# Retention in small steps queued behind Strassen products, the table of angles kept on chip, and part of the rotary sums on VectorE

## The chip, the cores and the metric

The kernel runs on one core of a Trainium2 chip. It is written in Bass with the Tile layer: the program names tiles and instructions, Tile places the tiles, adds the waits between engines, and fixes the order of each engine's instructions when the program is built. The metric is device time in microseconds of one execution. The engines are TensorE (PE; its weight loads PEld), VectorE (DVE), ScalarE (ACT), GpSimd (POOL) and SyncE (SP), which here issues nearly all DMAs.

## The reference

The reference is one inference step of a one-layer streaming encoder on 1024 prompt tokens and 64 sample tokens, 1088 in all, with a model width of 1024, in float32. What matters here is its first part, the input projection and the retention branch:

```
xn = rms_norm(x);  q, k, v, gate, swa_q, swa_k, swa_v, gate_a, gate_b = split(xn @ w_in)
q, k = rope(q), rope(k) / 16                  # 4 heads of 256, halves of 128: x1*cos - x2*sin, x2*cos + x1*sin
per chunk:  s = (q @ k.T) * decay             # inside the chunk
            o = s @ v + (q @ state) * q_decay
            state = state * gamma^C + (k * k_decay).T @ v
a = (rms_norm(o) * silu(gate)) @ w_ret_out
```

The states after the prompt and after the sample are outputs too. Sliding-window attention, the mixing of both branches, cross attention and a gated feed-forward part follow.

## The kernel before

All matmuls that carry float32 data are done in three passes: both operands are split into a high part (a cast on ACT) and a low part (a subtraction on DVE), by `split` at line 122, and high by high, high by low and low by high are summed in PSUM.

**Products.** The input projection goes by pairs of 128 output columns. A pair is one Strassen multiplication (`strassen`, line 247): seven products instead of eight, each of 24 matmuls (`multiply`, line 197) into two PSUM banks (`bank_pair`; three such pairs turn round). The weights are loaded as two raw tiles, POOL forms four sums of their quarters, ACT and DVE split seven results (`weight_ops`, line 166; five tiles for the split weights). DVE forms the running sums u2, u3, u5 and hands each of four quadrants of the result, i the column block and t the half of the tokens, to an `emit` function. Head 0's values are multiplied without Strassen (`plain`).

**What is done with a quadrant.** `project_phase` (line 541) holds four cases. `taken` (line 556) writes the quadrant into the next of eight stage tiles, in turn. `values` stores it to DRAM. `project` multiplies it by the token's inverse root mean square, on POOL, or on DVE where a sigmoid or SiLU on ACT follows. `rotated` (line 581) waits until both column blocks of a token half are there, loads the cosines and sines of that half (a tile `cs` of one buffer, line 590), forms two products with the sines in a tile `ab` and two with the cosines in place, all on DVE (lines 594 to 597), lets POOL subtract and add (lines 598 and 599), and stores both results to `d_qkv`.

**Retention.** `retention` (line 691) works on one head, four blocks of 256 tokens and then the 64 sample tokens. For a block it loads k, v and q from `d_qkv`, transposes k on PE and scales and splits it (`kt`, lines 709 to 715), splits k and q (`ks`, `qs`), transposes v and scales and splits it (`vb`), multiplies k by q (`pss`, line 725), masks and splits the scores (`sf`, `ss`), multiplies `kt` by `vb` (`pkv`, line 737), adds that to the state (line 747), and sums the output `po` from scores and values and from the queries and the old state (lines 748 to 758). `ret_out` (line 793) takes the output's squares on ACT, an inverse root through some small DVE and ACT instructions (`rsqrt`, line 280), scales it (line 808), transposes it back (`pb`, line 812) and stores it to `d_ret`. All of these PSUM tiles, and those of the roots, share two banks (`bank`, line 679, tag "r"). The working tiles, `ks`, `qs`, `vf`, `kt`, `vb`, `sf`, `ss`, `st`, `state` and `o`, have one buffer each.

**The order of the work.** The loop at line 628 goes over the four heads: k and q of the head with their rotation; for head 0 the tokens' squares (`token_squares`), roots (`token_roots`) and the decay tables (`retention_setup`); for the others v and the window queries of the head before (`w_sq`); then the retention of the head. After head 0, `spread_roots` writes the roots along the tokens, after head 1 `bias_table` builds the bias rows of the window attention. Behind the loop come the window keys and values, the last window queries, three sets of gates of four pairs each, and steps of the memory projection between them. That is the order of writing. Each engine's queue is ordered when the program is built, by a timeline of modelled durations: of the instructions whose inputs are ready in it, the one written first goes first. So the retention of a head, written before the next head's products, is ahead of them where it is ready, and they fill the time in which it is not. An engine takes its queue strictly in order on the chip. `issue_after(x)` adds that what is written under it, on the engine of x, comes after x; `in_order` (line 851) does that with the last matmul, and the window attention already uses it.

Of the kernel before, what the change touches and what calls it, by code (L numbers as in the profile page):

```python
# [29 lines left out]
H = 4  # L30
# [79 lines left out]
class Kernel:  # L110
    def __init__(self, nc, tc, io, decay):
        self.nc, self.tc, self.io, self.decay = nc, tc, io, decay
        self.later = []
        self.refill = None

# [340 lines left out]
    def token_roots(self):  # L456
# [4 lines left out]
        for i in range(9):  # L461
            w = P if i < 8 else SMP
            nc.tensor.matmul(pv[:w, i, :], self.rstd[:, i * P:i * P + w], self.ones[:, :2], start=True, stop=True)
# [3 lines left out]
    def spread_roots(self):  # L467

        for c0, n in ((0, 512), (512, 512), (1024, SMP)):
            pb = self.norm_psum("pb")  # L470
            for a in range(0, n, P):
                w, i = min(P, n - a), (c0 + a) // P
                self.nc.tensor.matmul(pb[:, a:a + w], self.rtok[:w, i:i + 1].broadcast_to([w, P]), self.ident[:w, :w],
                                      start=True, stop=True)
# [46 lines left out]
    def bias_table(self):  # L521
# [3 lines left out]
        rb = self.ra.tile([P, 2, BLK], F32, tag="o", bufs=1, name="rb")[:16, 0, :]  # L525
# [5 lines left out]
        nc.vector.tensor_copy(rb, pb[:16, :256])  # L531
        self.store(self.d_rb.rearrange("h (i c) -> h i c", c=256), rb.unsqueeze(1).broadcast_to([16, 64, 256]))
# [8 lines left out]
    def project_phase(self):  # L541
        nc, tc, io = self.nc, self.tc, self.io
        with ExitStack() as ctx:
# [11 lines left out]

            def taken(ps, sb):
                o = stage[count[0] % len(stage)]
                count[0] += 1
# [22 lines left out]
            def rotated(w, h, j):  # L581
# [3 lines left out]
                def emit(i, t, ps, sb):  # L585
# [8 lines left out]
                    tt(out=ab[:, 0, :], in0=a, in1=cs[:, 1, :], op=ALU.mult)  # L594
                    tt(out=ab[:, 1, :], in0=b, in1=cs[:, 1, :], op=ALU.mult)
                    tt(out=a, in0=a, in1=cs[:, 0, :], op=ALU.mult)
                    tt(out=b, in0=b, in1=cs[:, 0, :], op=ALU.mult)
                    nc.gpsimd.tensor_tensor(out=a, in0=a, in1=ab[:, 1, :], op=ALU.subtract)
                    nc.gpsimd.tensor_tensor(out=b, in0=b, in1=ab[:, 0, :], op=ALU.add)
# [21 lines left out]

            values(first, 0, self.plain)
# [3 lines left out]
            with ExitStack() as rctx:  # L626
                self.ra = rctx.enter_context(tc.tile_pool(name="ra", bufs=1, reuse_waits="tile"))
                for h in range(H):
                    rotated(pair("w_k", h) if h else first, h, 1)
                    if h == 0:  # L630
                        self.token_squares()
                    rotated(pair("w_q", h), h, 0)
                    if h == 0:
                        self.token_roots()
                        self.retention_setup()
                    else:
                        values(pair("w_v", h), h)
                    if h:
                        project(pair("w_sq", h - 1), queries(h - 1))
                    self.retention(h)  # L640
                    if h == 0:
                        self.spread_roots()
                    if h == 1:
                        self.bias_table()
# [4 lines left out]
            project(self.load_ops((io["w_sk"], io["w_sv"])), lambda i, t, o: self.store(self.d_skv[i, :, half(t)], o))  # L649
            project(pair("w_sq", 3), queries(3))  # L650
            steps = [0, 0, 0, 0, 1, 2, 2, 2, 3, 3, 2, 0]
            for idx, w, act in ((1, "w_ga", AF.Sigmoid), (0, "w_rg", AF.Silu), (2, "w_gb", AF.Sigmoid)):
                for m in range(0, KT, 2):
                    store = nc.scalar.dma_start if idx else self.store
                    put = lambda i, t, o, idx=idx, m=m, store=store: store(self.d_gate[idx][m + i, :, half(t)], o)
                    other = None if idx else lambda i, m=m: self.d_ret[m + i]
                    with tc.issue_after(project(pair(w, m // 2), put, act, other)):
                        for i in range(steps.pop(0)):
# [3 lines left out]
                            else:  # L662
                                next(memory)

# [17 lines left out]
    def turned(self, x, n):  # L682

        pk = self.bank("pk")
        for jt in range((n + P - 1) // P):
            w = min(P, n - jt * P)
            for dt in range(2):
                self.nc.tensor.transpose(pk[:w, jt, dt * P:(dt + 1) * P], x[:, dt, jt * P:jt * P + w], self.ident)
        return pk

    def retention(self, h):
# [9 lines left out]
        state = st = None  # L701
        for b in range(NBLK):
            c0 = b * BLK
            ks, qs, vf = pair("ks"), pair("qs"), new("vf")
            kraw, qraw = ks[:, 1].bitcast(F32), qs[:, 1].bitcast(F32)
            self.load(kraw, src(1, c0, BLK))
            self.load(vf, src(2, c0, BLK))
            self.load(qraw, src(0, c0, BLK))
# [11 lines left out]
            for jt in range(2):  # L720
# [3 lines left out]
                                               ALU.mult, ALU.subtract)  # L724
            pss = self.bank("pss")
# [10 lines left out]
            self.split(sf, ss[:, 0], ss[:, 1])  # L736
            pkv = self.bank("pkv")
# [11 lines left out]
            for it in range(2):  # L749
                for jt in range(it + 1):  # L750
# [865 lines left out]
```

## Time and profile before

| | |
|---|---|
| median of 3 runs | 2260.78 us (2258.72 to 2265.74) |
| the profiled execution | 2262.17 us, of which the span from the first to the last instruction is 2260.3 us |
| mean granted TensorE clock | 0.983 |
| PE busy | 2170.2 us, 96% of the span, 16580 matmuls |
| DVE busy | 1587.3 us, 70%, 2673 instructions |
| ACT busy | 896.4 us, 40%, 1923 |
| POOL busy | 691.1 us, 31%, 467 |
| DMA | 298.67 MB, on SP's queue all but 8.91 MB of the data and 2.70 MB of instructions |

The profile is of one execution. Busy time is the time in which an engine works on at least one instruction; matmuls overlap, so the time from the start of one to the start of the next says more of PE's pace than one matmul's duration. The granted clock is the share of TensorE's full clock that its throttle let through. A wait is put down to the instruction or the DMA that ended it. A tile's name stands with its line, as in "pb L812"; `pq` is the PSUM tile of a product, `wq` a split weight, `raw` a weight as loaded.

### The profile page before, as it was taken

To read this page: it belongs to the slowest core of one execution; us is meant where nothing else is said; L and a number is where in the kernel's file an instruction comes from. 1 tells how busy PE (TensorE), PEld (TensorE's weight loads), DVE (VectorE), ACT (ScalarE), POOL (GpSimd) and SP (SyncE) were. 2 spreads that over 40 slices of the span, in tenths; PEclk is the share of its full clock that TensorE was granted. 3 is DMA by queue.
4 is the path that set the end of the run, shared out by engine and by line. 5 is a ranking of instruction groups with operands and counts; after the bars stand their busy time and mean duration, and the time that the engine had idled before them with its cause. 6 is when DMAs were issued, how large, how long until landed. Compare 5 with 4: busy or idle time off the path is not lost.

```text
span 2260.3 us, 42100 instructions
## 1 busy us (share of the span) xinstructions
PE 2170.2 (96%) x16580; PEld 2117.9 (94%) x16580; DVE 1587.3 (70%) x2673; ACT 896.4 (40%) x1923; POOL 691.1 (31%) x467
## 2 busy tenths in 40 slices
PE   7999999999999989999999999999999999999996
PEld 6999998999999977889999998999999999999996
DVE  8986877766677657885455565776777677778497
ACT  7333333345444355553133343333222222344244
POOL 1441533242244112220000000014556555434462
PEclk9999999999999989999999999999999999999998
DMA  5644445443444466326443112422342332476233
GB/s 191 191 139 133 131 143 143 131 136 113 151 156 148 155 223 203 114 77 214 124 153 118 38 53 69 135 73 88 121 134 94 101 129 80 154 256 195 72 97 108
DMA packets 186408, 298.67 MB, mean 132 GB/s; under 512 B 40514, under 2 KB 111074, under 8 KB 186210
## 3 DMA queue, kind: packets, MB, share of 16 engines
q1 hardware_dynamic: 181602, 287.06, 40.4%
q10 hardware_dynamic: 4608, 8.91, 1.1%
q8 instruction: 131, 2.15, 0.4%
q14 instruction: 67, 0.55, 0.1%
HBM read 204.75 MB, written 91.16 MB: 131 GB/s over the span
## 4 chain that ended last, share of the span: by engine, by line
PE 77%; DVE 12%; DMA 5%; ACT 3%; issue 2%; POOL 1%; SPq 0%; DVEq 0%; ACTq 0%; POOLq 0%
PE pq L205 15%; PE pq L208 15%; PE pq L206 15%; PE pd L149 7%; PE pd L151 7%; PE pd L150 7%; DVE wq L124 2%; DVE B L124 1%; DVE T L124 1%; DMA cs<-c_rope 1%; PE pss L930 1%; DMA hl<-d_op 1%; PE pout L996 1%; PE pp L973 1%; DVE stage L562 1%
## 5 line engine op out<-in xcount | busy, mean ns | idle before, releaser
L123 ACT CAST wq<-raw 128x512 fp32r<-128x512 f32 (+1 forms) x509 | 310.2, 614 | 569.3 <-PE pq L208 289.3
L124 DVE TENSOR_TENSOR wq<-raw,wq 128x512 fp32r<-128x512 f32 (+1 forms) x509 | 450.3, 888 | 120.7 <-ACT wq L123 118.7
L205 PE MATMUL pq<-T,wq 128*128 128x272 f32 x1832 | 503.4, 292 | 4.1 <-DVE T L124 2.7
L206 PE MATMUL pq<-T,wq 128*128 128x272 f32 x1832 | 499.7, 289 | 0.0
L205 PE MATMUL pq<-B,wq 128*128 128x272 f32 x1592 | 439.2, 293 | 11.3 <-ACT wq L123 10.2
L206 PE MATMUL pq<-B,wq 128*128 128x272 f32 x1592 | 437.3, 291 | 9.1 <-DVE B L124 8.9
L208 PE MATMUL pq<-T,wq 128*128 128x272 f32 x1832 | 384.5, 290 | 0.7 <-DVE wq L124 0.6
L183 POOL TENSOR_TENSOR raw<-raw 128x512 f32<-128x512 f32 (+1 forms) x59 | 81.2, 1377 | 890.2 <-DVE wq L124 665.7
L205 PEld LDWEIGHTS pq<-T,wq 128*128 128x128 f32 x1832 | 347.3, 190 | 5.4 <-ACT wq L123 3.6
L206 PEld LDWEIGHTS pq<-T,wq 128*128 128x128 f32 x1832 | 350.6, 191 | 0.3 <-issue 0.3
L208 PE MATMUL pq<-B,wq 128*128 128x272 f32 x1592 | 333.9, 290 | 0.0
L206 PEld LDWEIGHTS pq<-B,wq 128*128 128x128 f32 x1592 | 305.9, 192 | 11.8 <-DVE B L124 11.4
L205 PEld LDWEIGHTS pq<-B,wq 128*128 128x128 f32 x1592 | 303.0, 191 | 12.0 <-ACT wq L123 10.2
L208 PEld LDWEIGHTS pq<-T,wq 128*128 128x128 f32 x1832 | 287.2, 190 | 2.2 <-DVE wq L124 1.5
L208 PEld LDWEIGHTS pq<-B,wq 128*128 128x128 f32 x1592 | 250.1, 190 | 0.5 <-issue 0.3
L252 DVE TENSOR_TENSOR u<-pq,u 128x544 f32<-128x544 f32 x177 | 127.5, 720 | 121.8 <-PE pq L208 121.1
L186 POOL TENSOR_TENSOR raw<-raw 128x512 f32<-128x512 f32 (+1 forms) x59 | 83.2, 1410 | 126.1 <-DVE wq L124 118.4
L562 DVE TENSOR_TENSOR stage<-pq,u 128x544 f32<-128x544 f32 x112 | 80.2, 716 | 28.4 <-PE pq L208 28.3
L958 POOL TENSOR_TENSOR t<-t,den 128x768 f32<-128x768 f32 (+2 forms) x34 | 47.8, 1406 | 145.7 <-DVE den L956 58.4
L184 POOL TENSOR_TENSOR raw<-raw 128x512 f32<-128x512 f32 (+1 forms) x59 | 87.2, 1477 | 3.7
L1450 POOL TENSOR_TENSOR y<-u,y 128x544 f32<-128x544 f32 x38 | 63.3, 1674 | 72.8 <-DVE y L1448 52.9
L189 POOL TENSOR_TENSOR raw<-raw 128x512 f32<-128x512 f32 (+1 forms) x59 | 83.7, 1418 | 4.5
(361 smaller groups left out, 4662.6 us busy)
## 6 DMA issues: line engine op xcount, KB each, us to landing
hl<-d_op SPq DMA_DIRECT2D x85, 272.0 KB, 4.3
d_qkv<-stage SPq DMA_DIRECT2D x44, 272.0 KB, 4.4
d_op<-stage SPq DMA_DIRECT2D x44, 272.0 KB, 2.3
d_op<-ht SPq DMA_DIRECT2D x44, 272.0 KB, 3.5
raw<-w_gate SPq DMA_DIRECT2D x22, 512.0 KB, 3.5
raw<-w_up SPq DMA_DIRECT2D x22, 512.0 KB, 4.3
cs<-c_rope SPq DMA_DIRECT2D x16, 544.0 KB, 4.4
d_gate<-stage ACTq DMA_DIRECT2D x32, 272.0 KB, 2.5
```

The lines of the kernel that those rows point to most:

```text
L123: self.last_cast = self.nc.scalar.copy(hi, src).ins
L124: self.nc.vector.tensor_tensor(out=lo, in0=src, in1=hi.bitcast(F32), op=ALU.subtract)
L149: mm(ps, wh, xh, start=start, stop=False)
L150: mm(ps, wh, xl, start=False, stop=False)
L151: self.last_mm = mm(ps, wl, xh, start=False, stop=stop).ins
L184: tt(out=a21, in0=a21, in1=a22, op=add)
L189: tt(out=a12, in0=a12, in1=a11, op=sub)
L205: mm(ps[:, c, :HC], w[:, 0, ks], x[:, 0, cs], start=start, stop=False)
L206: mm(ps[:, c, :HC], w[:, 0, ks], x[:, 1, cs], start=False, stop=False)
L208: self.last_mm = mm(ps[:, c, :HC], w[:, 1, ks], x[:, 0, c * HC:(c + 1) * HC], start=False, stop=stop).ins
L252: add = lambda out, a, b: nc.vector.tensor_tensor(out=out, in0=a, in1=b, op=ALU.add)
L562: nc.vector.tensor_tensor(out=o, in0=ps, in1=sb, op=ALU.add)
```

## The change

- `product` can put its matmuls in order behind the last matmul, and then takes one step from a generator, `side`, whose PE instructions come in order behind the product. From head 1 on, the generator is the retention of the head before (`retention_steps`), and the 28 products of a head (k, q, v, window queries) take one step each; what is left is taken at the end of the head (`finish_side`). The last head's retention goes along with the window keys and values, the last window queries and two pairs of the first gate, which are moved ahead of the memory phase for that.
- `retention` becomes such a generator. A block has five steps: the transposes of k and v with their splits; the scores, behind them the back-transposes of the block before and the load of the next keys and values; `pkv` and the state; `po`, the load of the next queries and the split of the state; and a step that issues nothing. The sample has five: its loads, then transposes, scores, outputs and the last back-transposes. For head 0 four steps go ahead, with the roots, the decay tables and `spread_roots` in them.
- In `po` the terms with the state come first.
- `ret_out` is cut in two: `ret_scaled` up to the scaled output, `ret_turn` with the transposes and the store.
- The table of cosines and sines for all tokens is loaded once into a tile `rope` and stays; `cs` and `ab` go. The products with the sines take two of the eight stage tiles.
- The final subtraction and addition of the rotation are on DVE for heads 0 and 1, on POOL for the others.
- `bias_table` stores its rows in pieces of 512 columns instead of 256.

The diff, cut to its core:

```diff
     def product(self, w, x, name, operand):
-        ps = self.multiply(self.bank_pair(), w[name], x[operand])
+        if self.side is None:
+            ps = self.multiply(self.bank_pair(), w[name], x[operand])
+        else:
+            ps = self.in_order(lambda: self.multiply(self.bank_pair(), w[name], x[operand]))
+            self.in_order(lambda: next(self.side, None))
...
-        self.store(self.d_rb.rearrange("h (i c) -> h i c", c=256), rb.unsqueeze(1).broadcast_to([16, 64, 256]))
+        for i in range(2):
+            nc.vector.tensor_copy(rb[:, i, :], pb[:16, :256])
+        rb = rb.rearrange("h i c -> h (i c)")
+        self.store(self.d_rb.rearrange("h (i c) -> h i c", c=512), rb.unsqueeze(1).broadcast_to([16, 32, 512]))
...
-                    cs = self.ra.tile([P, 2, HALF], F32, tag="cs", bufs=1, name="cs")
-                    self.load(cs, io["c_rope"][:, :, half(t)])
-                    ab = self.ra.tile([P, 2, HALF], F32, tag="ab", bufs=1, name="ab")
+                    cos, sin = (rope[:, i, half(t)] for i in range(2))
+                    sa, sb = turn(), turn()
                     tt = nc.vector.tensor_tensor
...
+                    tt(out=sb, in0=b, in1=sin, op=ALU.mult)
+                    tt(out=sa, in0=a, in1=sin, op=ALU.mult)
+                    tt(out=a, in0=a, in1=cos, op=ALU.mult)
+                    tt(out=b, in0=b, in1=cos, op=ALU.mult)
+                    add = (nc.vector if h < 2 else nc.gpsimd).tensor_tensor
+                    add(out=a, in0=a, in1=sb, op=ALU.subtract)
+                    add(out=b, in0=b, in1=sa, op=ALU.add)
...
+                rope = self.ra.tile([P, 2, T], F32, name="rope")
+                self.load(rope, io["c_rope"])
+                rotated(first, 0, 1)
+                self.token_squares()
+                rotated(pair("w_q", 0), 0, 0)
+                for h in range(1, H):
+                    self.side = self.retention_steps(h - 1)
+                    rotated(pair("w_k", h), h, 1)
+                    rotated(pair("w_q", h), h, 0)
+                    values(pair("w_v", h), h)
+                    project(pair("w_sq", h - 1), queries(h - 1))
+                    self.finish_side()
+                self.side = self.retention_steps(H - 1)
+                project(self.load_ops((io["w_sk"], io["w_sv"])), lambda i, t, o: self.store(self.d_skv[i, :, half(t)], o))
+                project(pair("w_sq", 3), queries(3))
+                for m in (0, 2):
+                    gate_columns(1, "w_ga", AF.Sigmoid, m)
+                self.finish_side()
...
+    def finish_side(self):
+        for _ in range(64):
+            if self.in_order(lambda: next(self.side, True)):
+                break
+        self.side = None
+
+    def retention_steps(self, h):
+        if h == 0:
+            yield
+            self.token_roots()
+            self.retention_setup()
+            yield
+            yield
+            self.spread_roots()
+            yield
+        yield from self.retention(h)
+        if h == 1:
+            yield
+            self.bias_table()
...
+        keys, queries = load_keys(0), load_queries(0)
         for b in range(NBLK):
...
+            (ks, vf), qs = keys, queries
...
+            yield
             pss = self.bank("pss")
...
             self.split(sf, ss[:, 0], ss[:, 1])
+            if out is not None:
+                self.ret_turn(*out)
+            if b < NBLK - 1:
+                keys = load_keys(b + 1)
+            yield
             pkv = self.bank("pkv")
...
+            yield
             po = self.bank("po")
...
             if b < NBLK - 1:
+                queries = load_queries(b + 1)
                 st = pair("st")
                 self.split(state, st[:, 0], st[:, 1])
-            self.ret_out(h, po, 2 * b, c0, BLK)
+            out = self.ret_scaled(h, po, 2 * b, b * BLK, BLK)
+            yield
+            yield
...
+        yield
+        self.ret_turn(*out)
         kv = ra.tile([P, 2, BLK], F32, tag="kt", bufs=1, name="kvs")
...
+        yield
         pss = self.bank("psss")
...
+        yield
         po = self.bank("pos")
...
-        self.ret_out(h, po, 8, SEQ, SMP)
+        out = self.ret_scaled(h, po, 8, SEQ, SMP)
+        yield
+        self.ret_turn(*out)
```

More of the change, by code (lines that the diff above doesn't have):

```diff
@@ L554, in project_phase, with next_stage @@
             flat = lambda o: o.rearrange("p b c -> p (b c)")
+            def next_stage():
+                count[0] += 1
+                return stage[(count[0] - 1) % len(stage)]
+            turn = lambda: flat(next_stage())
             def taken(ps, sb):
[L557 to L558 removed]
+                o = next_stage()
                 if sb is None:
@@ L648, in project_phase @@
             memory = self.memory_phase(mp)
-            project(self.load_ops((io["w_sk"], io["w_sv"])), lambda i, t, o: self.store(self.d_skv[i, :, half(t)], o))
-            project(pair("w_sq", 3), queries(3))
-            steps = [0, 0, 0, 0, 1, 2, 2, 2, 3, 3, 2, 0]
+            steps = [0, 0, 1, 2, 2, 2, 3, 3, 2, 0]
             for idx, w, act in ((1, "w_ga", AF.Sigmoid), (0, "w_rg", AF.Silu), (2, "w_gb", AF.Sigmoid)):
[L653 to L657, printed above, removed]
+                for m in range(4 if idx == 1 else 0, KT, 2):
+                    with tc.issue_after(gate_columns(idx, w, act, m)):
                         for i in range(steps.pop(0)):
```

80 lines of the change are left out of this document (37 added, 43 removed).

## The prediction

> **What bounds the kernel now.** I read the page first, then the busy time by stretches, the waits of PE, the waits of DVE and ACT, and last the timeline around single waits.
>
> ```profile
> span 2260.3 us, 42100 instructions
> ...
> PE   7999999999999989999999999999999999999996
> ...
> PEclk9999999999999989999999999999999999999998
> ```
>
> PE is busy in nearly all of the 40 slices, so the kernel ends when PE has done its matmuls. Nothing is to be won but PE's idle time and the time in which its clock is granted at less than full speed. The change touches the first quarter, so I asked for stretches there: 85.3:592 runs from the matmuls for the roots to the last head's last transposes, that is over all of retention, 600:800 holds products without retention, and the next five hold the long waits.
>
> ```profile
> 85.30:592.00 506.70, 487.55 (x3779) 475.45 (x3778) 375.67 (x677) 204.34 (x434) 176.13 (x117) 0.98 0.45 133
> 600.00:800.00 200.00, 200.00 (x1608) 199.84 (x1607) 145.57 (x196) 83.89 (x142) 66.55 (x44) 1.00 0.47 153
> ...
> 86.00:95.50 9.50, 7.27 (x38) 6.85 (x37) 8.94 (x10) 3.61 (x5) 7.39 (x6) 0.64 0.11 29
> 112.00:119.20 7.20, 4.77 (x26) 4.26 (x25) 5.70 (x8) 1.44 (x3) 3.13 (x3) 0.76 0.19 62
> 252.00:259.20 7.20, 5.01 (x30) 4.85 (x29) 6.20 (x12) 2.99 (x6) 1.09 (x1) 0.76 0.93 275
> 376.00:385.50 9.50, 4.94 (x25) 4.72 (x24) 8.45 (x17) 2.67 (x7) 2.92 (x2) 0.64 0.68 204
> 410.00:416.20 6.20, 3.73 (x19) 3.65 (x19) 4.75 (x11) 1.89 (x4) 0.28 (x1) 0.72 0.92 324
> ```
>
> After the length come PE, PEld, DVE, ACT and POOL, each busy time with its count, then the granted clock, the DMA share and GB/s. Undisturbed, PE starts 1608 matmuls in 200 us, one each 0.124 us; a product of 24 is 3.0 us. In the retention stretch PE idles 506.70 - 487.55 = 19.2 us. In the five short stretches the clock is also low (0.64 to 0.76). They last 39.6 us and hold 138 matmuls, which need 138 x 0.124 = 17.1 us; so 22.5 us are lost there, 13.9 of them idle (39.6 - 25.72 busy) and 8.6 by the slow clock. The idle time outside them is 19.2 - 13.9 = 5.3 us. Together 27.8 us can be had in this stretch, and no more. Who ends the idle time:
>
> ```profile
> PE pb L812 <- ACT ret_o L808: 11.7, 7, 4.6
> PE pss L149 <- ACT qs L123: 2.3, 1, 2.3
> PE pk L688 <- DMA ks<-d_qkv: 1.9, 1, 1.9
> PE pk L688 <- issue: 1.6, 1, 1.6
> ...
> PE pss L149 <- DVE kt L714: 0.3, 1, 0.3
> ```
>
> PE waits mostly for the scaled output of a retention block (total, times, longest), though the products around it are independent: the order on PE was fixed for other durations than the chip's. What makes that output late stands in the waits of DVE and ACT and in the timeline before the longest wait:
>
> ```profile
> DVE ab L594 <- DMA cs<-c_rope: 11.6, 5, 4.5
> ```
> ```profile
> ACT kt L713 <- DVE kt L714: 18.6, 12, 5.3
> ...
> ACT qs L123 <- DMA qs<-d_qkv: 9.8, 7, 2.3
> ```
> ```profile
> 371.39 0.73 DVE L594 TENSOR_TENSOR ab<-stage,cs 128x544 f32<-128x544 f32 x1 [4.52 <-DMA cs<-c_rope]
> ...
> 376.32 1.81 DVE L124 TENSOR_TENSOR st<-state,st 128x512 fp32r<-128x512 f32 x1
> ...
> 380.45 0.91 ACT L808 ACTIVATE ret_o<-ret_o,rr 128x256 f32<-128x256 f32 x2 [1.30 <-DVE rr L298]
> ...
> 381.02 0.69 PE L812 MATMUL pb<-ident,ret_o 128*128 128x128 f32 x2 [4.56 <-ACT ret_o L808]
> ```
>
> DVE stood 4.52 us at a rotation that waited for its angles; the state's split and the root queued behind it, ACT scaled at 380.45, and PE stood 4.56 us. One load of angles cost one 4.6 us wait and its slow clock.
>
> **The change, part by part.** The table of angles on chip removes DVE's 11.6 us of waits for cs. The one load that stays is 1088 KB, two pieces in one.
>
> ```profile
> 44.18 0.67 SPq L117 DMA_DIRECT2D cs<-c_rope  x1
> ...
> 60.70 1.82 DVE L595 TENSOR_TENSOR ab<-stage,cs 128x544 f32<-128x544 f32 x1
> ```
> ```profile
> d_qkv<-stage SPq DMA_DIRECT2D x44, 272.0 KB, 4.4
> ...
> cs<-c_rope SPq DMA_DIRECT2D x16, 544.0 KB, 4.4
> ```
>
> A piece lands after 4.4 us, so the table after some 9, issued at 44, where the first piece was; the first rotation came at 60. That hides it. Without that cover, weights queued behind it on SP would come some 4 us later, once.
>
> The fixed order puts two or three products (6 to 9 us) between a block's steps where it matters: the next keys are loaded four products ahead, the next queries two. That takes the waits for ks, qs and issue, and gives the scaled output three products, eight transposes and the twelve matmuls of pss, 9.0 + 1.0 + 1.5 = 11.5 us, before its own transposes. On SP the next keys stand behind the store of the output (L814's copy), with the same four products to spare. I count the whole 27.8 us as removed, and the new waits against it. No retention matmul is added or dropped; the gate products that move ahead ran beside the last head's retention before as well, at no cost.
>
> New wait one: the scores step has one product of cover. After the transposes of k (and 0.5 us of v's) comes one product, 3.0 us, and then pss, which needs both halves of kt out of the PSUM bank and ks split.
>
> ```profile
> 549.44 0.38 PE L688 MATMUL pk<-ident,ks 128*128 128x128 f32 x2
> ...
> 550.83 0.68 DVE L124 TENSOR_TENSOR ks<-ks 128x512 fp32r<-128x512 f32 x1
> ...
> 552.65 0.48 DVE L714 SCALAR_TENSOR_TENSOR kt<-pk,tok,kt 128x256 fp32r<-128x256 f32 x1
> ```
> ```profile
> 355.13 0.60 PE L688 MATMUL pk<-ident,ks 128*128 128x128 f32 x4
> ...
> 356.88 1.78 DVE L124 TENSOR_TENSOR ks<-ks 128x512 fp32r<-128x512 f32 x1
> ...
> 360.96 0.48 DVE L714 SCALAR_TENSOR_TENSOR kt<-pk,tok,kt 128x256 fp32r<-128x256 f32 x1
> ```
>
> In the first block, with no rotation near, kt is done 553.13 - 549.82 = 3.3 us after the transposes, inside the 3.5 us of cover; in the second, with rotations and a ks split of 1.78 instead of 0.68, after 361.44 - 355.73 = 5.7 us, 2.2 over. Behind pss on PE stand the next product and all others. Bounds for 16 blocks: 0 and 35 us. By the new count of steps about four blocks (the second of two heads, one or two more) open beside a rotation: four at 2.2, twelve at 0, is 8.8 us.
>
> New wait two: in the sample's first step pb, k's and v's transposes follow without a product between, on two banks, so v's wait until DVE has copied pb out.
>
> ```profile
> L814 DVE COPY ret_t<-pb 128x512 f32<-128x512 f32 x16 | 10.9, 683 | 2.6 <-PE pb L812 2.6
> ```
>
> 0.68 for the copy and 0.2 for the hand-overs, less 0.2 of k's transposes, is 0.7 a head, 2.8 us (2 to 8 if DVE is busy).
>
> New wait three: head 0 has four more steps, so its last transposes come right behind the sample's matmuls, without a product. They wait for the root's chain:
>
> ```profile
> 216.26 0.64 PE L785 MATMUL pos<-kvs,sfs 64*64 64x256 f32 x2
> ...
> 216.84 1.13 PE L788 MATMUL pkvs<-kvs 64*128 64x256 f32 x4
> ...
> 219.59 0.51 ACT L808 ACTIVATE ret_o<-ret_o,rr 64x256 f32<-64x256 f32 x1 [1.52 <-DVE rr L298]
> ```
>
> 220.1 - 216.9 = 3.2 us, less 1.0 of pkvs: 2.2 us, once (0 to 5, with a slow clock after it). The other heads have a product there.
>
> New wait four: rotations now take eight of the eight stage tiles, so tile 0 is wanted by the next call's second product while its store may be under way.
>
> ```profile
> L562 DVE TENSOR_TENSOR stage<-pq,u 128x544 f32<-128x544 f32 x73 | 52.2, 715 | 11.2 <-PE pq L208 11.2
> ...
> L596 DVE TENSOR_TENSOR stage<-stage,cs 128x544 f32<-128x544 f32 x16 | 14.9, 934 | 0.0
> ```
> ```profile
> L598 POOL TENSOR_TENSOR stage<-stage,ab 128x544 f32<-128x544 f32 x16 | 28.8, 1802 | 53.6 <-DVE stage L596 42.0 <-DVE rv L805 10.9 <-DVE rs_t L292 0.7
> ```
>
> From the last product: 0.7 + 3 x 0.93 + 1.8 + 4.4 = 9.7 us, against two products and their steps, 8 us. So DVE would stand some 1.7 us, eight times, with weight splits and kt behind it. PE has three pairs of banks and can run two more products (6 us) meanwhile: 0, and at most 8 x 1.7 = 14 us if that cover is used up.
>
> The first heads' sums on DVE: sixteen passes of about 0.72, 11.5 us more on DVE, against sixteen of 1.8 off POOL, beside which DVE's own passes stretch.
>
> ```profile
> 45.00:85.30 40.30, 40.20 (x320) 39.99 (x320) 38.05 (x49) 19.75 (x33) 18.85 (x11) 1.00 0.76 243
> ```
>
> DVE is 94% busy in head 0 and PE does not wait. Half of the 11.5 falls here; the squares' sums that fill this stretch become due two products (6 us) later than before, and cover it. Cost 0; up to 3 us if not, and a gain of as much if POOL's stretch goes. The bias rows' store in pieces of twice the size, and the order within po, lie beside other work: 0.
>
> Sum: -27.8 + 8.8 + 2.8 + 2.2 = -14.0 us. The profiled execution took 2262.2 us (span 2260.3 and 1.9 around it), 1.4 above the median of the runs; 2262.2 - 14.0 - 1.4 = 2246.8 us.
>
> The clock is weighed once more. In the five short stretches above it fell with 2.2, 2.4, 2.2, 4.6 and 2.5 us of idle time. [...]
>
> **Rivals.** Slower: the scores step waits in every block. One mechanism, kt's chain of ACT and DVE hops on a shared bank, behind weight splits and rotations. At 2.2 us a block it is 35 us, with the other new waits 40 - 27.8 = +12: 2273. Since 2.2 us was enough to drop the clock, and a drop of 0.24 x 7.2 = 1.7 us came with each, it may reach +39: 2300. It decides from (27.8 - 5) / 16 = 1.4 us a block. For it: ACT's 18.6 us at kt, and POOL's stretching of ks. Against: pss waited 0.3 us for kt in the whole stretch before.
>
> Same: the stage tiles' wait reaches PE, 14 us back: 2261.
>
> Not what it says: the scaled output stays late for another reason (queries landing late hold ACT for 9.8 us), so pb's 11.7 us stay, and the clock of its three stretches, 22.9 us with 74 matmuls: 22.9 - 13.7 busy is 9.2 idle, 13.7 - 74 x 0.124 is 4.5 by the clock. 27.8 - 16.2 - 13.8 is -2.2: 2263.
>
> Better: no new wait shows: 2233.
>
> **How the numbers follow.** This kernel's runs tell 0.3%, 6.8 us, from no change. Forecast, up to 2254: 0.50, and the better case 0.16. Not what it says: 0.07, and stage tiles: 0.11, both inside 0.3%. Slower: 0.16, from 2268 on. So faster 0.66, same 0.18, slower 0.16. The range runs from 2232, the better case, to 2270, which leaves out most of the slower rival.
>
> **What would show it.** Right: no wait of DVE on cs; pb's waits on ret_o near 0; 0 or 1 slow clock stretches in retention instead of five; pss waits on kt of 5 to 12 us in all; v's transposes waiting on the copy four times; retention's stretch some 14 us shorter. Wrong: pss or pk among the longest waits at every block; L562 waiting on d_qkv's store; the clock still low in several stretches, or the time moved to stages after 800 us.

## The result, and the profile after

The change made the kernel slower. Four executions of the changed kernel took 2276.1 us (median, 2275.1 to 2278.6), four of the kernel before on the same chip 2262.0; the ratio is 1.0067, 95% interval 1.0053 to 1.0081. The forecast was 2246.8 us, range 2232 to 2270.

The page of the changed kernel, PE by slices:

```profile
span 2273.9 us, 42109 instructions
...
PE   7998998999999998999999999999999999999997
...
PEclk9999999999999999999999999999999999999998
```

A slice is 57 us. PE has an 8 in the fourth and the seventh slice now (171 to 227 us and 341 to 398 us), both inside retention, where it had only 9s. The clock row, a mean over slices, is too coarse for stretches of a few us. How much is lost there, the first scores of the window attention tell: everything before them is projection and retention. In the timeline of the kernel before they start here,

```profile
825.33 0.55 PE L930 MATMUL pss<-swin,swin 64*128 64x64 f32 x6
```

and in that of the changed kernel here:

```profile
840.13 0.55 PE L998 MATMUL pss<-swin,swin 64*128 64x64 f32 x6 [0.82 <-DVE stage L575]
```

That is 14.8 us later; from there to the end both take the same (1434.9 and 1433.8 us). So the loss lies wholly in the stretch that the change touches. PE's waits there, from 45 us on (in all, times, longest):

```profile
PE pss L150 <- DVE kt L760: 19.0, 12, 6.4
PE pk L723 <- DVE ret_t L882: 5.5, 4, 3.7
PE pb L879 <- ACT ret_o L869: 2.4, 2, 2.2
PE pb L479 <- DVE rtok L299: 2.2, 1, 2.2
PE pb L879 <- DVE vb L769: 2.2, 2, 1.7
```

The 11.7 us of `pb` on the scaled output are 2.4 now, and no wait on queries, keys or their loads is left. In their place stands 19.0 us at the scores, which wait for `kt`. The busy time by short stretches, at and just behind four of the longer waits (lengths and columns as in the prediction's stretches):

```profile
104.00:109.00 5.00, 4.41 (x22) 4.07 (x23) 5.00 (x19) 1.71 (x4) 3.31 (x2) 0.66 0.41 132
206.00:213.00 7.00, 3.69 (x17) 3.65 (x18) 5.01 (x8) 0.62 (x1) 5.99 (x5) 0.63 0.36 97
223.00:229.00 6.00, 5.40 (x31) 5.33 (x32) 0.29 (x1) 0.75 (x2) 0.00 (x0) 0.72 0.27 76
378.00:384.00 6.00, 2.90 (x12) 2.64 (x12) 6.00 (x11) 1.46 (x3) 3.06 (x2) 0.54 0.12 46
```

The clock is 0.54 to 0.72 there: four slow stretches in retention instead of five. The clock's own record has stretches of 3.4 or 6.8 us at half speed (a granted clock of 0.5) here, 20.4 us of them between 45 us and the window attention; before it had 23.8.

Why `kt` is late can be seen before the longest wait, in the timeline of the changed kernel (the transposes of k ended at 370.9):

```profile
373.44 0.47 ACT L759 ACTIVATE kt<-pk,tok 128x256 fp32r<-128x256 f32 x1
...
374.17 0.72 DVE L606 TENSOR_TENSOR stage<-stage,rope 128x544 f32<-128x544 f32 x1
...
374.33 1.68 POOL L187 TENSOR_TENSOR raw<-raw 128x512 f32<-128x512 f32 x1 [4.36 <-DVE wq L125]
...
374.93 1.67 DVE L609 TENSOR_TENSOR stage<-stage,rope 128x544 f32<-128x544 f32 x1
...
376.52 0.71 DVE L575 TENSOR_TENSOR stage<-pq,u 128x544 f32<-128x544 f32 x1
...
377.15 1.11 DVE L125 TENSOR_TENSOR ks<-ks 128x512 fp32r<-128x512 f32 x1
378.19 0.47 DVE L760 SCALAR_TENSOR_TENSOR kt<-pk,tok,kt 128x256 fp32r<-128x256 f32 x1
...
378.70 0.47 ACT L759 ACTIVATE kt<-pk,tok 128x256 fp32r<-128x256 f32 x1 [1.66 <-DVE kt L760]
...
380.21 0.47 DVE L760 SCALAR_TENSOR_TENSOR kt<-pk,tok,kt 128x256 fp32r<-128x256 f32 x1
...
380.83 0.55 PE L150 MATMUL pss<-qs,ks 128*128 128x256 f32 x1 [6.45 <-DVE kt L760]
```

ACT starts on `kt` only 2.5 us after the transposes, behind the scaling of the block before's output and the cast of a weight. It has `kt`'s first high part out at 373.9, but DVE takes its low part at 378.2: two passes of a rotation, one sum of a product and the split of k are queued ahead of it, and the second of them takes 1.67 us beside a POOL pass. ACT goes on with the second half only behind that, and PE, in its fixed order, stands behind the scores. From the end of k's transposes to the end of `kt` it takes 2.75 to 3.02 us in four of the sixteen blocks, 3.79 to 5.34 in eleven, and 9.75 in this one. The cover, the time that PE's work in between takes, is 3.3 to 3.5 us.

The chain was not faster in the kernel before. There it took 2.5 to 8.1 us in fifteen of the blocks, over 3.5 in eight of them, and 18.5 in head 0's first block, where `kt` waited for the decay tables. But the planned order had 4.8 to 7.8 us of other work on PE ahead of the scores of those fifteen (22.5 in the first), more where `kt` was later, and PE waited there only 0.3 us in all. The longest of the fifteen, in the timeline of the kernel before:

```profile
159.57 0.38 PE L688 MATMUL pk<-ident,ks 128*128 128x128 f32 x2
...
167.53 0.47 DVE L714 SCALAR_TENSOR_TENSOR kt<-pk,tok,kt 128x256 fp32r<-128x256 f32 x1
...
168.06 0.39 PE L149 MATMUL pss<-qs,ks 128*128 128x256 f32 x1 [0.27 <-DVE kt L714]
```

### The profile page after: what moved, and what is told of

Its sections match the earlier page's. It is cut to its first block, busy times and chain, and to the rows that moved or that the text cites. A ratio compares the mean times of both kernels' runs of the same rounds, so it can differ in the third digit from the quotient of the medians.

```text
span 2273.9 us, 42109 instructions
## 1 busy us (share of the span) xinstructions
PE 2172.8 (96%) x16580; PEld 2119.9 (93%) x16580; DVE 1583.2 (70%) x2690; ACT 894.5 (39%) x1921; POOL 666.2 (29%) x451
## 4 chain that ended last, share of the span: by engine, by line
PE 77%; DVE 11%; DMA 5%; ACT 4%; issue 3%; POOL 1%; SPq 1%; DVEq 0%; ACTq 0%; POOLq 0%
PE pq L206 15%; PE pq L209 15%; PE pq L207 15%; PE pd L150 7%; PE pd L152 7%; PE pd L151 7%; DVE wq L125 2%; PE pss L998 1%; DMA hl<-d_op 1%; DVE B L125 1%; PE pout L1064 1%; ACT wq L124 1%; DVE stage L575 1%; DMA qs<-d_qkv 1%; DVE T L125 1%
```

## The experiments

**Theories.** First: the scores step has too little cover, one product, and the whole loss follows from that. Rival: DVE is overloaded by the sums moved to it and the stage tiles' reuse, and the waits only show where PE happens to stand. Second rival: the steps at a head's end, with the slow clock behind their waits, are most of it.

All kernels in one table. "Idle" is PE's, from 45 us to the first scores of the window attention; "half clock" is the length of the record at half speed in that stretch; both come from the profiled execution. The ratio is that of 4 to 11 executions to the kernel before on the same chip. The sets ran on several chips, so small differences between two rows are better read from the ratios than from the medians.

| kernel | median us | ratio, 95% interval | scores wait for kt | idle | half clock | window attention at |
|---|---|---|---|---|---|---|
| before | 2260.2 to 2262.7 | 1 | 0.3 | 19.2 | 23.8 | 825.3 |
| changed | 2276.1 | 1.0067 (1.0053 to 1.0081) | 19.0 | 33.2 | 20.4 | 840.1 |
| no cover | 2342.7 | 1.0361 (1.0347 to 1.0375) | 64.8 | 73.9 | 78.2 | 902.0 |
| empty step moved | 2254.0 | 0.9967 (0.9954 to 0.9980) | 3.9 | 13.7 | 10.2 | 816.8 |
| sums on POOL | 2284.7 | 1.0097 (1.0081 to 1.0112) | 20.0 | 37.1 | 23.8 | 843.9 |
| ends apart | 2280.2 | 1.0082 (1.0069 to 1.0094) | 27.8 | 35.0 | 23.8 | 840.3 |
| moved, ends re-ordered | 2248.9 | 0.9946 (0.9934 to 0.9958) | 3.6 | 9.4 | 13.6 | 812.4 |
| the same, v apart | 2256.3 | 0.9978 (0.9967 to 0.9990) | 2.9 | 15.4 | 17.0 | 819.0 |
| the same, third product | 2249.0 | 0.9946 (0.9934 to 0.9959) | 2.1 | 9.2 | 3.4 | 809.5 |
| third product, all sums on DVE | 2248.0 | 0.9947 (0.9934 to 0.9959) | 1.4 | 7.7 | 6.8 | 810.0 |
| before + table | 2248.9 | 0.9945 (0.9933 to 0.9958) | 0 | 15.1 | 3.4 | 813.5 |
| before + table + two heads' sums | 2247.0 | 0.9939 (0.9925 to 0.9954) | 0 | 11.1 | 6.8 | 810.1 |
| before + all sums | 2242.2 | 0.9913 (0.9897 to 0.9929) | 0.3 | 6.7 | 6.8 | 805.6 |
| before + table + all sums | 2239.6 | 0.9899 (0.9885 to 0.9913) | 0 | 5.2 | 3.4 | 804.6 |

### The scores step's cover

**The empty step moved.** One line goes up:

```diff
+            yield
             yield
             pss = self.bank("pss")
...
             out = self.ret_scaled(h, po, 2 * b, b * BLK, BLK)
             yield
-            yield
```

> The changed kernel with one edit: the step that issues nothing stands between a block's transposes and its scores, and no longer behind the block's output. The scores step then has two products of cover (6.5 us) and every other distance keeps its length or loses one of four. First theory, the changed kernel is slow because kt's chain of ACT and DVE passes needs 2.8 to 5.3 us and the scores step gives it 3.5: PE's wait at pss for kt falls from 19.0 us to about 3 (only the block where kt took 9.75 us is still late), and 14 to 19 us go, to 2257 to 2262. Second theory, DVE has too much work around the rotations (sums moved to it, stage tiles that wait for their stores): the same work is only awaited elsewhere (vb, ss, the products' banks), pss's wait is replaced by others, and less than 5 us go: 2271 or more.

2254.0 us, 22.1 less than the changed kernel. PE's waits behind 45 us:

```profile
PE pss L150 <- DVE kt L760: 3.9, 3, 3.4
PE pb L879 <- ACT ret_o L869: 3.8, 3, 2.2
PE pk L723 <- DVE kvs L830: 1.8, 3, 1.0
```

The instructions on DVE, ACT and POOL are the same; the order on PE differs, and with it part of the planned order on DVE and ACT. The 15 us at the scores are gone and came up nowhere else: the first theory holds and the overload does not. The gain is larger than expected since 10.2 us of half clock went with the waits.

**No cover.** The opposite edit, the scores in the same step as the transposes:

```diff
-            yield
             pss = self.bank("pss")
...
             out = self.ret_scaled(h, po, 2 * b, b * BLK, BLK)
             yield
             yield
+            yield
```

> The changed kernel with the scores directly behind the block's transposes, in one step, and two steps that issue nothing behind the output. First theory: kt's chain takes what it took (69.9 us from the transposes' ends to kt's, over 16 blocks), nothing of it is covered but v's transposes, so PE waits 50 to 65 us at the scores instead of 19, the clock falls in more stretches, and the time is 2310 to 2340. Second theory (the steps' waits only move about, DVE sets the pace): less than 15 us are added: 2280 to 2291.

```profile
PE pss L150 <- DVE kt L760: 64.8, 16, 8.9
```

2342.7 us, a little above what was expected. So the wait goes 64.8, 19.0, 3.9 us with none, one and two products between, behind a cover of 0.4, 3.3 and 6.3 us. The lags of `kt` over the sixteen blocks add up to 69.4, 69.9 and 76.8 us: the chain does not get shorter, the cover decides. The time beyond the waits is mostly the clock: 15 slow stretches, 78.2 us at half speed.

### The parts of the change one by one

**Before + table.** In the kernel before, only the angles:

```diff
-                    cs = self.ra.tile([P, 2, HALF], F32, tag="cs", bufs=1, name="cs")
-                    self.load(cs, io["c_rope"][:, :, half(t)])
-                    ab = self.ra.tile([P, 2, HALF], F32, tag="ab", bufs=1, name="ab")
+                    cos, sin = (rope[:, i, half(t)] for i in range(2))
+                    sa, sb = turn(), turn()
...
+                rope = self.ra.tile([P, 2, T], F32, name="rope")
+                self.load(rope, io["c_rope"])
```

> The kernel before with only the table of angles on chip (scratch from the stage tiles, order of the products of the rotation as in the changed kernel, sums on POOL), and the retention not in fixed steps but placed as before. If the late angles are what makes pb late, as forecast, DVE's 11.6 us of waits go, pb's wait falls from 11.7 us to some 3, and the time falls by 8 to 20 us: 2242 to 2254. If the scaled output is late for another reason, pb's wait stays near 11 us and the time at 2258 to 2265. If the stage tiles' reuse costs, DVE waits at the stage tiles for their stores for over 5 us in all and the time is 2262 to 2275.

```profile
PE pb L818 <- ACT ret_o L814: 6.1, 5, 1.6
PE pk L694 <- issue: 4.7, 1, 4.7
```

2248.9 us, 13.7 less than the kernel before. `pb`'s wait is 6.1 us (some 3 were expected), none over 1.6; the half clock falls from 23.8 to 3.4 us. The 4.7 us at `pk` come once, in head 0, and the trace names nothing that PE waited for; the one slow stretch follows them. This kernel's order is planned anew when the program is built, as in every kernel here without steps, and that is part of what is measured.

**Sums on POOL.** The changed kernel with `add = nc.gpsimd.tensor_tensor` for every head.

> The changed kernel with the rotation sums of the first two heads back on POOL, nothing else. First theory (kt's chain has too little cover in every head): nothing that can be told, 2273 to 2279; pss waits 17 to 21 us for kt, as in heads 2 and 3, where the sums were on POOL anyway. Second theory (DVE is overloaded by the sums): the waits of 105:230 fall, most of all the 2.2 us at the spreading of the roots, and 5 to 10 us go: 2266 to 2271.

```profile
PE pss L150 <- DVE kt L760: 20.0, 12, 6.0
...
PE pq L206 <- DVE u L257: 3.9, 1, 3.9
```

2284.7 us, 8.6 more than the changed kernel by the medians, some 6.8 by the ratios, whose intervals touch: both theories missed the time, and beside these steps DVE's sums are no loss but a gain of a few us. In the profiled executions 3.8 us of it lie before the window attention, the rest behind it, where no rotation runs; why, stays open. Set against the kernel with the table alone, which ran on the same chip, this one differs by the fixed steps and what goes with them: 2284.7 - 2248.9 = 35.8 us is their price with the sums on POOL.

### The ends of a head

**Ends apart.** The changed kernel with the output's transposes in a step of their own ahead of the sample's, and head 0's last output kept for head 1:

```diff
         self.ret_turn(*out)
+        yield
         kv = ra.tile([P, 2, BLK], F32, tag="kt", bufs=1, name="kvs")
...
-        yield
-        self.ret_turn(*out)
+        if h == 0:
+            self.held = out
+        else:
+            yield
+            self.ret_turn(*out)
...
+        if h == 1:
+            yield
+            self.ret_turn(*self.held)
+            yield
         yield from self.retention(h)
```

> The changed kernel with the steps at a head's end set apart: in the sample's first step the output's transposes stand one product ahead of those of k and v, and head 0's last output is turned in head 1's second step instead of directly behind the sample's matmuls. The scores step keeps its one product. First theory (the scores step's cover is the main cost): the waits at the sample's v (5.5 us) and at head 0's last pb (2.2) go with one or two of the four slow clock stretches, 6 to 11 us, to 2265 to 2270, and the 19 us at pss stay. Rival (these ends, and the slow clock behind their waits of 3.7 and 2.2 us, are most of the loss): 12 us or more go, to 2264 or below.

```profile
PE pss L150 <- DVE kt L764: 27.8, 12, 7.5
...
PE pb L887 <- ACT ret_o L877: 0.7, 1, 0.7
```

2280.2 us, a miss for both. The waits at the ends went as wanted, but head 1's blocks came two products later, two of them beside other work: there the scores waited 4.7 and 4.9 us, where the changed kernel waited 1.7 and 0.7. With one product of cover, what falls beside a block decides, and this edit re-dealt it.

**Moved, ends re-ordered.** Both at once, with no step more: the sample's loads go with the last block's output, its k and v are transposed first, the last output one product behind, and head 0's last output with head 1's first scores.

```diff
             out = self.ret_scaled(h, po, 2 * b, b * BLK, BLK)
-            yield
-            yield
+            if b < NBLK - 1:
+                yield
...
         yield
-        self.ret_turn(*out)
         kv = ra.tile([P, 2, BLK], F32, tag="kt", bufs=1, name="kvs")
...
         yield
+        self.ret_turn(*out)
+        yield
         pss = self.bank("psss")
...
-        out = None
+        out = self.held if h == 1 else None
```

> The empty step moved as before (two products of cover for the scores), and the steps at a head's end re-ordered without one more step: the sample's loads go with the last block's output, its k and v are transposed first, the last block's output is transposed one product behind them, and head 0's last output is turned with the scores of head 1's first block. First theory (each wait of PE is one distance that is too short): of the 13.7 us that PE still idles behind 45 us in the kernel with the moved step, the 6 us at the sample and at the last output go, with one or two of the three slow clock stretches: 2244 to 2249. Rival, seen when the ends alone were set apart (waits there went, 9 us came back at the scores, because a head's blocks moved to other products): no gain with two products of cover either, 2252 or more.

2248.9 us, at the end of what was expected: PE idles 4.3 us less than with the moved step alone, and one wait of note is left (3.1 us), with 6.8 us at half clock behind it. The other 6.8 us follow the small matmuls of the roots, with waits of 0.6 and 0.7 us only. The wait:

```profile
PE pss L150 <- DVE kt L760: 3.6, 3, 3.1
```

**The same, v apart.** v's transposes go into the empty step:

```diff
+            yield
             pv = self.turned(vf, BLK)
...
             yield
-            yield
             pss = self.bank("pss")
```

> The kernel with the moved step and the re-ordered ends, and the transposes of v put into the step that issues nothing, one product behind those of k. If the passes that turn v out of its bank stand between kt's own passes on DVE and make it late, kt is done sooner, the one block that waits 3.4 us waits under 1.5, and 2 to 4 us go beside the kernel with the moved step and ends. If kt is late by rotations and weight splits ahead of it on DVE, it is as late as before and the two kernels agree within 2 us, or this one is slower by a wait of the state's update for v's passes.

```profile
PE pb L884 <- DVE sf L782: 5.5, 2, 3.2
PE pss L150 <- DVE kt L760: 2.9, 2, 2.6
PE pb L884 <- DVE vb L770: 2.3, 3, 1.0
```

2256.3 us. `kt` is nearly as late in the block that waits (8.9 us after the transposes, 9.4 without the edit), so v's passes are not what makes it late. The loss, 7.4 us, is more than expected: the output's transposes behind the scores now wait, 2.3 us for v's bank, which is drained later, and 5.5 us until DVE has taken the scores out of theirs. Why the second grew was not tested; in both cases v's last pass stands right behind on DVE.

**The same, third product.** `if b == 1 and h: yield` ahead of the scores.

> The kernel with the moved step and the re-ordered ends (2248.9, where the scores still waited 3.1 us in head 2's second block, with 6.8 us of half clock behind it), with one more step that issues nothing ahead of the scores in the second block of heads 1 to 3, which have steps to spare. First theory (cover decides): no wait at any scores step is over 0.5 us, one slow stretch in retention instead of two, and 3 to 6.5 us go: 2242 to 2246. Rival (a block that moves by a product meets other work, as when the ends alone were set apart): waits of over 1 us come up at other blocks and the time stays at 2247 or more.

2249.0 us against 2248.9: no gain that can be told, so the first theory missed the time, though no wait over 1 us came up at another block's scores either. The step did what it was to do (no scores wait over 0.7 us, 3.4 us of half clock instead of 13.6, the window attention 2.9 us earlier), but the profiled execution took 2.2 us longer behind that point, with 60.4 us at half clock there instead of 53.4. Why, stays open.

### The sums on VectorE

**Before + table + two heads' sums**, which is the change without its steps.

> The kernel before with the table on chip and the sums of the first two heads on DVE: all of the change but the fixed steps. Beside the table alone (2248.9). If the sums on DVE are a gain by themselves (the changed kernel lost 8.6 us when they went back to POOL), 2238 to 2245. If that loss was only a matter of where the steps fell, as most of it came after retention's end, the two agree within 4 us: 2245 to 2253.

2247.0 us: the same as the table alone, within the intervals. Set against the changed kernel, it gives the price of the steps in the change as it stands: 2276.1 - 2247.0 = 29.1 us, and the ratios, 1.0067 and 0.9939, say the same. The table and these sums gain 14 us, the steps lose 29. With the moved step and the re-ordered ends (0.9946) the loss is gone, but nothing is gained by the steps either.

**Third product, all sums on DVE**, `add = nc.vector.tensor_tensor` for every head.

> The same, with the rotation sums of all four heads on DVE. If POOL's passes stretch DVE's beside them (a root's pass over 128x2 took 642 ns on the mean, 1.25 us beside POOL), and the changed kernel's 8.6 us for two heads were a real gain, kt and the root are done sooner in heads 2 and 3 and 2 to 8 us go beside the kernel with the third product. If DVE, busy for 573 of 767 us, becomes what the products wait for, waits on u, stage and kt rise and it is slower by up to 10 us.

2248.0 us, the same as with two heads' sums, where 2 to 8 us less were expected. Idle fell to 7.7 us, and again more half clock stood behind (70.5 us).

**Before + table + all sums.**

> The kernel before with the table on chip and the sums of all four heads on DVE, no fixed steps. Beside 2247.0 with two heads' sums on DVE and 2248.9 with none, which did not differ: if the sums on DVE are worth nothing by themselves where the steps are placed freely, 2243 to 2252; if POOL's sharing is the larger cost, 2236 to 2243; if DVE is then full, 2252 to 2262.

2239.6 us, ratio 0.9899 (0.9885 to 0.9913): the fastest here, faster than both kernels of the case. The same parts with the repaired steps took 2248.0 us (ratio 0.9947); why the steps cost so much there was not traced.

**Before + all sums**, the angles loaded as before:

```diff
-                    nc.gpsimd.tensor_tensor(out=a, in0=a, in1=ab[:, 1, :], op=ALU.subtract)
-                    nc.gpsimd.tensor_tensor(out=b, in0=b, in1=ab[:, 0, :], op=ALU.add)
+                    nc.vector.tensor_tensor(out=a, in0=a, in1=ab[:, 1, :], op=ALU.subtract)
+                    nc.vector.tensor_tensor(out=b, in0=b, in1=ab[:, 0, :], op=ALU.add)
```

> The kernel before with the rotation sums of all four heads on DVE and nothing else: the angles are still loaded for each rotation. The table alone took 13.7 us off, the table and these sums 21 to 23. If the two are worth about the same alone as together, the sums alone take 5 to 10 us off: 2252 to 2257, and DVE still waits some 10 us for angles. If late angles undo what the sums give (DVE stands at a load with the sums queued behind it), the time is 2259 to 2266. If the sums are most of it and late angles would do no harm beside them, 2242 to 2249.

```profile
PE pb L812 <- ACT ret_o L808: 2.9, 1, 2.9
```
```profile
DVE ab L594 <- DMA cs<-c_rope: 7.3, 6, 3.5
```

2242.2 us. DVE still waits 7.3 us for angles, and yet `pb` waits 2.9 instead of 11.7. So this does not add up with the table: either edit takes most of the same slow stretches (23.8 us at half clock before, 3.4 and 6.8 with either). By the ratios they are worth 12 us (table) and 20 us (sums), and both together 23.

## Why the prediction was wrong

The reading of what bounds the kernel held: nothing but PE's waits and its clock moved the time, and the loss is theirs. The sum failed at these steps.

| term | forecast | measured |
|---|---|---|
| old waits of PE in retention | -19.2 | gone |
| slow clock | -8.6 | 23.8 to 20.4 us at half speed: -1.7 |
| scores wait for kt | +8.8 | +19.0 |
| sample's v waits for the copy | +2.8 | +5.5 |
| head 0's last output | +2.2 | +2.4 of pb, 2.2 of it there |
| stage tiles, sums on DVE | 0 | no wait of PE; the sums -7 to -9 here, 0 without the steps |
| not foreseen | | roots +2.2, pb on vb's bank +2.2, u +0.9 |

**The cover of the scores, "new wait one", is the step that failed.** The mechanism was named and its bounds, 0 and 35 us, held. The size was taken from two lags of the kernel before, 3.3 and 5.7 us, as "four at 2.2, twelve at 0". Twelve blocks waited, 1.6 us on the mean. Two lags and a count of rotations stood for sixteen lags. In the same trace eight of fifteen were over 3.5 us, and behind a cover of 3.45 us the fifteen would have waited 14.1 us, an estimate from their lags. The row of ACT at `kt`, 12 waits and 18.6 us, pointed there, but went to the rival alone. What was held against that rival, 0.3 us of waiting at the scores, came from the planned order's cover of 4.8 to 7.8 us and not from a short chain. The rest, from 14.1 to 19.0, came with the new order; which work beside the blocks made it was not tested. The slower rival gave exactly this mechanism and decided from 1.4 us a block; 1.2 (19.0 over sixteen blocks) was enough since the clock came back as well. It got 0.16.

**"I count the whole 27.8 us as removed"** failed for its second part. The slow stretches did not belong to the old waits alone: four came behind the new waits of 2.2, 3.7, 2.2 and 6.4 us, and I had charged the new waits no clock.

**New waits two and three** were right in place; the longest of the four at v is 3.7 us, because DVE's weight split and two product sums of 0.7 us stood ahead of the copy there. **Stage tiles:** right, DVE waits for them this long in all of 85 to 600 us, and PE not:

```profile
DVE stage L575 <- DMA d_qkv<-stage: 1.4, 2, 0.9
```

**The table** was right in place: no wait on angles is left, and alone it gives 13.7 us. **The sums** at 0, with a bound of 3, were sized too small beside the steps, where they gain some 7 to 9 us; without the steps two heads' sums gain nothing that can be told, and those of all heads 20 us alone and some 10 beside the table. The stretching of DVE beside POOL was in the text, as a gain of "as much".

**The other rivals** fell: `pb`'s waits did go, and the stage tiles did not hold PE.

**Not added up:** idle in retention +14.0, the clock there -1.7, in the start stage -0.7 idle and +1.7 by the clock; that is 13.3 of the 14.8 us before the window attention. Some 1.5 us, perhaps PE's pace where steps and products meet, weren't traced. The profiled executions differ by +13.6 us (2275.7 against 2262.2) where the sum had -14.0. Of these 27.6 us the scores are 10.2, the clock in retention 6.9, the waits not foreseen 5.3 and the sample's v 2.7; so the cover is the largest term, and not the only one.

## What to carry to other kernels

Before fixing an order, measure every lag of each chain that it must cover, not one or two of them, and how much cover the old order gave it; and place the slack where the wait would stand on the critical engine: the same empty step cost or saved 22 us by its place alone. An order planned by readiness had hidden these lags here, and the steps' own price, 29 us, ate the 14 us that the other two parts gain; so time each part of a change alone. Where an engine's passes take longer beside another's, as DVE's splits of a weight did here beside POOL (1170 ns on the mean, 671 to 696 without), moving work between the two can be free: look at busy time of both before and after (here POOL -52.9 us and DVE -4.6), not at the sum of the passes moved (22.7 us).

## What the runs showed of the hardware

**DVE beside POOL.** Busy time from 45 us to the window attention, in the kernel before (PE, PEld, DVE, ACT, POOL with counts, then clock, DMA share, GB/s),

```profile
45.00:825.00 780.00, 760.75 (x5967) 748.28 (x5967) 576.94 (x942) 317.61 (x625) 271.88 (x178) 0.98 0.48 148
```

and in that with the table and all sums on DVE:

```profile
45.00:804.00 759.00, 754.45 (x5987) 743.65 (x5985) 572.33 (x975) 319.99 (x628) 218.98 (x147) 1.00 0.45 142
```

POOL lost 52.9 us. DVE took 32 sums more, 22.7 us by their rows, and is busy 4.6 us less. Where part of that comes from, the groups on DVE show (busy, mean ns), before,

```profile
L562 DVE TENSOR_TENSOR stage<-pq,u 128x544 f32<-128x544 f32 x108 | 77.3, 716 | 24.4 <-PE pq L208 24.3
...
L124 DVE TENSOR_TENSOR qs<-qs 128x512 fp32r<-128x512 f32 x16 | 14.9, 929 | 5.8 <-ACT qs L123 5.7
L124 DVE TENSOR_TENSOR st<-state,st 128x512 fp32r<-128x512 f32 x12 | 13.8, 1153 | 10.0 <-ACT st L123 10.0
```

and after:

```profile
L567 DVE TENSOR_TENSOR stage<-pq,u 128x544 f32<-128x544 f32 x110 | 78.8, 717 | 25.2 <-PE pq L208 18.1 <-DMA d_qkv<-stage 6.8
...
L124 DVE TENSOR_TENSOR qs<-qs 128x512 fp32r<-128x512 f32 x16 | 11.6, 725 | 6.6 <-ACT qs L123 6.6
L604 DVE TENSOR_TENSOR stage<-stage 128x544 f32<-128x544 f32 x16 | 11.4, 712 | 0.0
L603 DVE TENSOR_TENSOR stage<-stage,stage 128x544 f32<-128x544 f32 x16 | 11.3, 712 | 0.0
L124 DVE TENSOR_TENSOR st<-state,st 128x512 fp32r<-128x512 f32 x12 | 8.3, 690 | 17.8 <-ACT st L123 17.8
```

A pass that reads one operand from PSUM takes 716 or 717 ns in both. The two splits, with both operands in SBUF, took 929 and 1153 ns on the mean before and take 725 and 690 after; the sums, which are on DVE only after, take 712. Pass by pass, in the trace of the kernel before: of the splits of a weight between 45 and 800 us (128x512), 115 ran with no POOL instruction beside them and took 671 to 696 ns; 72 ran beside one and took 1170 on the mean, up to 1853. What makes a pass longer there was not tested. The sums alone, moved from POOL to DVE, took about 20 us off (2242.2 us, ratio 0.9913).

**The order.** In the trace of the kernel before, DVE's 2673 and POOL's 467 instructions, and those of PE and ACT too, stand in the order of the built program, told by the tiles they write and read.

**The clock.** In the fourteen traces, between 60 and 800 us, I took PE's waits over 0.5 us with no other within 7 us. Of 70 under 1.8 us none was followed by a half clock stretch; of 22 of 1.8 to 3.0 us, 17 were; of 24 over 3.0 us, 22. The stretch starts some 1 to 5 us after the wait's start and lasts 3.4 us or a multiple. So in these traces a lone wait of 2 us cost 2 us and mostly 1.7 more (half of 3.4), an estimate from these counts and lengths. Single long waits are not all of it: of the 51 slow stretches in these traces eight have no wait of 1.8 us in the 7 us before them. Seven of the eight follow the small matmuls of the roots and a wait of 0.7 us; what lowers the clock there was not tested.
